# Instance norm over 65,536 rows: loads and stores moved to one queue in one fixed order, rows computed one by one

The kernel runs on one core of one Trainium2 chip. The metric is the device time of one execution in microseconds (us), lower is better. All runs quoted are fast-state runs. The engines are named as the profiler does: SP (SyncE) and ACT (ScalarE) issue transfers, DVE (VectorE) computes the statistics, ACT normalises; the 16 DMA engines move the data.

## The reference

```python
def reference(x, eps):                     # x: 256 x 256 x 4096, float32; eps = 1e-5
    mean = np.mean(x, axis=2, keepdims=True)
    var = np.var(x, axis=2, keepdims=True)
    return ((x - mean) / np.sqrt(var + eps)).astype(np.float32)
```

1.07 GB are read and 1.07 GB written; arithmetic per element is small.

## The kernel before

256 tiles of 128 partitions x 2 rows x 4096 (4 MB). Six buffers (192 KB of each partition). Loads are issued by SP, stores by ACT, so they stand in two DMA queues.

```python
    P, K, BUFS = 128, 2, 6
    io = ...tile_pool(name="io", bufs=BUFS)
    small = ...tile_pool(name="small", bufs=2 * BUFS)
    # ... (cut: shapes, eps_tile)
    for i in range(ntiles):
        x_tile = io.tile([P, K, d], mybir.dt.float32)
        nc.sync.dma_start(out=x_tile, in_=x_t[i])
        # ... (cut: small tiles)
        for r in range(K):
            for j in range(nsub):                         # 8 pieces of 512
                nc.vector.bn_stats(out=stats[:, r, j, :], in_=xr[:, r, j, :])
            nc.vector.bn_aggr(out=mv[:, r, :], in_=stats[:, r])
        nc.scalar.activation(out=rstd, in_=mv[:, :, 1], func=Sqrt, bias=eps_tile, scale=1.0)
        nc.vector.reciprocal(out=rstd, in_=rstd)
        nc.vector.scalar_tensor_tensor(out=nbias, ...)    # -mean * rstd
        for r in range(K):
            nc.scalar.activation(out=x_tile[:, r, :], in_=x_tile[:, r, :], func=Identity,
                                 bias=nbias[:, r : r + 1], scale=rstd[:, r : r + 1])
        nc.scalar.dma_start(out=out_t[i], in_=x_tile)
```

The order of the source need not be the order on an engine: in this kernel's trace the reciprocal of tile 1 stands behind 12 statistics of tile 2.

## Time and profile before

| | before |
|---|---|
| median, range | 5180.1 us, 5177.9 to 5187.5 |
| DMA engines, share of the span taken by packets | 99.2% |
| DVE, ACT busy | 51%, 38% |
| mean rate over 200 to 5000 us | 416 GB/s |
| a transfer, issue to landing (median) | load 23.7 us, store 18.6 us |
| packets' time beyond 1213 ns each, mean of an engine | 164 us |

A tile must be moved in and out: 16 packets of 32,768 bytes on each of the 16 DMA engines. At 1213 ns a packet that is 19.4 us per tile. Before, a tile takes 20.2 us. The prediction reads the rest of this profile. The last row of the table comes from the trace's packet records. One more quantity, which the prediction did not look at, will matter: a transfer's landing is told by 16 semaphore steps, read here as one from each engine (8192 steps and 8192 four-byte packets for 512 transfers). The time from the first step to the last is called the *spread* here. In the kernel before its median is 1.4 us and its largest value 5.1 us, so the engines go in step.

These are the two lines of the DMA issues (from issue to landing in the last column):

```profile
x_tile<-in_x_dram SPq DMA_DIRECT2D x256, 4096.0 KB, 23.7
out_dram<-x_tile ACTq DMA_DIRECT2D x256, 4096.0 KB, 18.6
```

A 4 MB transfer alone takes 9.7 us of packets, and two that share the engines some 19.4. So each queue holds little more than the one transfer that is moving.

### The profile page before, as it was taken

How to read it: one execution, taken by the hardware profiler on the slowest of the kernel's cores; microseconds unless marked ns; L12 is line 12 of the kernel's file. 1: busy time of each engine (PE TensorE's matmuls, PEld its weight loads, DVE VectorE, ACT ScalarE, POOL GpSimd, SP SyncE). 2: the span in 40 equal slices, each digit the busy share in tenths (PEclk: the TensorE clock that was granted, in tenths of full speed). 3: DMA queues.
4: the chain of work that ended last, by engine and by line, in shares of the span. 5: the costliest groups of instructions: out<-in, count | busy, mean ns of one | idle time of the engine just before them, and what ended most of it. 6: DMA issues, size and time to landing. Idle time of an engine off the chain costs nothing.

```text
span 5180.7 us, 7450 instructions
## 1 busy us (share of the span) xinstructions
DVE 2654.0 (51%) x5121; ACT 1967.0 (38%) x769; POOL 0.2 (0%) x4
## 2 busy tenths in 40 slices
DVE  6544555554455555444555554455555445555543
ACT  3333333433333433433343433333343333334334
POOL 0000000000000000000000000000000000000000
DMA  9999999999999999999999999999999999999998
GB/s 425 412 410 413 420 417 422 417 414 416 410 416 413 417 418 414 413 412 417 417 416 418 413 414 418 410 417 420 417 415 417 417 413 417 417 419 415 415 416 367
DMA packets 73786, 2147.99 MB, mean 415 GB/s; under 512 B 8192, under 2 KB 8192, under 8 KB 8192
## 3 DMA queue, kind: packets, MB, share of 16 engines
q1 hardware_dynamic: 36864, 1073.76, 49.7%
q10 hardware_dynamic: 36864, 1073.76, 49.5%
q14 instruction: 58, 0.48, 0.0%
HBM read 1073.74 MB, written 1073.74 MB: 415 GB/s over the span
## 4 chain that ended last, share of the span: by engine, by line
DMA 69%; DVE 17%; ACT 7%; issue 6%; another core or an unknown queue 0%; SPq 0%
DMA x_tile<-in_x_dram 43%; DMA out_dram<-x_tile 26%; DVE stats L55 16%; ACT x_tile L77 7%; DVE mv L56 1%; DVE nbias L67 0%; SPq L46 0%; DVE rstd L65 0%; ACT rstd L58 0%
## 5 line engine op out<-in xcount | busy, mean ns | idle before, releaser
L55 DVE BATCH_NORM_STATS2 stats<-x_tile 128x6 f32<-128x512 f32 x4096 | 2464.1, 674 | 2460.3 <-DMA x_tile<-in_x_dram 2460.3
L77 ACT ACTIVATE x_tile<-x_tile,nbias,rstd 128x4096 f32<-128x4096 f32 x512 | 1917.8, 3793 | 3172.3 <-DVE nbias L67 3172.3
L56 DVE BATCH_NORM_AGGREGATE mv<-stats 128x2 f32<-128x48 f32 x512 | 185.7, 363 | 8.8
L58 ACT ACTIVATE rstd<-mv,eps_tile 128x2 f32<-128x2 f32 x256 | 71.7, 280 | 23.9 <-DVE mv L56 23.9
L67 DVE SCALAR_TENSOR_TENSOR nbias<-mv,rstd 128x2 f32<-128x2 f32 x256 | 41.0, 160 | 8.8
L65 DVE RECIPROCAL rstd<-rstd 128x2 f32<-128x2 f32 x256 | 27.7, 108 | 23.6 <-ACT rstd L58 23.6
L58 ACT ACT_TABLE_LOAD x1 | 1.3, 1283 | 0.7 <-PEq L101 0.7
L42 DVE MEMSET eps_tile<- 128x1 f32 x1 | 0.1, 59 | 0.8 <-PEq L101 0.8
L101 POOL MEMSET const-bfloat16-1.0<- 128x1 bf16 x1 | 0.1, 101 | 0.0
L101 POOL MEMSET const-uint8-127<- 128x1 uint8 x1 | 0.1, 101 | 0.0
L101 POOL MEMSET const-float32-0.0<- 128x1 f32 x1 | 0.1, 98 | 0.2 <-issue 0.2
L101 POOL MEMSET const-float32-1.0<- 128x1 f32 x1 | 0.1, 98 | 0.0
## 6 DMA issues: line engine op xcount, KB each, us to landing
x_tile<-in_x_dram SPq DMA_DIRECT2D x256, 4096.0 KB, 23.7
out_dram<-x_tile ACTq DMA_DIRECT2D x256, 4096.0 KB, 18.6
```

Of the source, the lines that this page charges most:

```text
L42: nc.vector.memset(eps_tile, eps)
L55: nc.vector.bn_stats(out=stats[:, r, j, :], in_=xr[:, r, j, :])
L56: nc.vector.bn_aggr(out=mv[:, r, :], in_=stats[:, r])
L58: nc.scalar.activation(out=rstd, in_=mv[:, :, 1], func=mybir.ActivationFunctionType.Sqrt, bias=eps_tile, scale=1.0,)
L65: nc.vector.reciprocal(out=rstd, in_=rstd)
L67: nc.vector.scalar_tensor_tensor(out=nbias, in0=mv[:, :, 0], scalar=-1.0, in1=rstd, op0=mybir.AluOpType.mult, op1=mybir.AluOpType.mult,)
L77: nc.scalar.activation(out=x_tile[:, r, :], in_=x_tile[:, r, :], func=mybir.ActivationFunctionType.Identity, bias=nbias[:, r : r + 1], sca ...
L101: nc = _bacc.Bacc("TRN2", target_bir_lowering=False, num_devices=1)
```

## The change

Its intent: one queue (SP's) for everything, in the fixed order store i, load i+4, so that directions alternate in 4 MB blocks and a load never waits for the store just issued. Sqrt, reciprocal and bias are done row by row.

```diff
+    AHEAD = 4
-    small = ...tile_pool(name="small", bufs=2 * BUFS)
+    small = ...tile_pool(name="small", bufs=8)
-    for i in range(ntiles):
+    def load(i):
         x_tile = io.tile([P, K, d], mybir.dt.float32)
         nc.sync.dma_start(out=x_tile, in_=x_t[i])
+        tiles[i] = x_tile
+    def row(x_tile, r):       # one row: 8 bn_stats, bn_aggr, sqrt, reciprocal, nbias, identity
+        ...                   # (cut: the same operations on [P, 1] in place of [P, K])
+    def finish(i):
+        x_tile = tiles.pop(i)
         for r in range(K):
-            ...
-        nc.scalar.dma_start(out=out_t[i], in_=x_tile)
+            row(x_tile, r)
+        nc.sync.dma_start(out=out_t[i], in_=x_tile)
+    for i in range(AHEAD):
+        load(i)
+    for i in range(ntiles):
+        finish(i)
+        if i + AHEAD < ntiles:
+            load(i + AHEAD)
```

More of the change, by code (lines that the diff above doesn't have):

```diff
@@ L25 @@
     n, d = x_flat.shape
-    rows_per_tile = P * K
-    assert n % rows_per_tile == 0
-    ntiles = n // rows_per_tile
+    ntiles = n // (P * K)
+    assert n == ntiles * P * K
     x_t = x_flat.rearrange("(t p k) d -> t p k d", p=P, k=K)
     out_t = out_flat.rearrange("(t p k) d -> t p k d", p=P, k=K)
-    BN_FMAX = nc.vector.BN_STATS_FMAX
-    nsub = (d + BN_FMAX - 1) // BN_FMAX
-    assert d % BN_FMAX == 0
+    FMAX = nc.vector.BN_STATS_FMAX
+    nsub = d // FMAX
+    assert d == nsub * FMAX
     io = ctx.enter_context(tc.tile_pool(name="io", bufs=BUFS))
-    small = ctx.enter_context(tc.tile_pool(name="small", bufs=2 * BUFS))
+    small = ctx.enter_context(tc.tile_pool(name="small", bufs=8))
     singles = ctx.enter_context(tc.tile_pool(name="singles", bufs=1))
@@ L42 @@
     nc.vector.memset(eps_tile, eps)
-    for i in range(ntiles):
+    tiles = {}
+    def load(i):
         x_tile = io.tile([P, K, d], mybir.dt.float32)
         nc.sync.dma_start(out=x_tile, in_=x_t[i])
-        stats = small.tile([P, K, nsub, 6], mybir.dt.float32)
-        mv = small.tile([P, K, 2], mybir.dt.float32)
-        rstd = small.tile([P, K], mybir.dt.float32)
-        nbias = small.tile([P, K], mybir.dt.float32)
+        tiles[i] = x_tile
+    def row(x_tile, r):
         xr = x_tile.rearrange("p k (s f) -> p k s f", s=nsub)
-        for r in range(K):
-            for j in range(nsub):
-                nc.vector.bn_stats(out=stats[:, r, j, :], in_=xr[:, r, j, :])
-            nc.vector.bn_aggr(out=mv[:, r, :], in_=stats[:, r])
+        stats = small.tile([P, nsub, 6], mybir.dt.float32)
+        mv = small.tile([P, 2], mybir.dt.float32)
+        rstd = small.tile([P, 1], mybir.dt.float32)
+        nbias = small.tile([P, 1], mybir.dt.float32)
+        for j in range(nsub):
+            nc.vector.bn_stats(out=stats[:, j, :], in_=xr[:, r, j, :])
+        nc.vector.bn_aggr(out=mv, in_=stats)
         nc.scalar.activation(
             out=rstd,
-            in_=mv[:, :, 1],
+            in_=mv[:, 1:2],
             func=mybir.ActivationFunctionType.Sqrt,
@@ L68 @@
             out=nbias,
-            in0=mv[:, :, 0],
+            in0=mv[:, 0:1],
             scalar=-1.0,
@@ L74 @@
         )
-        for r in range(K):
-            nc.scalar.activation(
-                out=x_tile[:, r, :],
-                in_=x_tile[:, r, :],
-                func=mybir.ActivationFunctionType.Identity,
-                bias=nbias[:, r : r + 1],
-                scale=rstd[:, r : r + 1],
-            )
-        nc.scalar.dma_start(out=out_t[i], in_=x_tile)
+        nc.scalar.activation(
+            out=x_tile[:, r, :],
+            in_=x_tile[:, r, :],
+            func=mybir.ActivationFunctionType.Identity,
+            bias=nbias,
+            scale=rstd,
+        )
+    def finish(i):
+        x_tile = tiles.pop(i)
+        for r in range(K):
+            row(x_tile, r)
[6 more added lines that the diff above has]
+            load(i + AHEAD)
 _INS = ['x', 'eps']
```

## The prediction

> **What bounds the kernel now.** I read the front page first: busy shares, the DMA rows, the queues.
>
> ```profile
> DVE 2654.0 (51%) x5121; ACT 1967.0 (38%) x769; POOL 0.2 (0%) x4
> ...
> q1 hardware_dynamic: 36864, 1073.76, 49.7%
> q10 hardware_dynamic: 36864, 1073.76, 49.5%
> ```
>
> No compute engine is near its limit. The two DMA queues (q1 the loads, q10 the stores) hold the 16 DMA engines for 49.7 + 49.5 = 99.2% of 5180.7 us. The kernel is bound by DMA time, so it can gain only if packets take less time or if the last 0.8% of idleness goes. Bytes do not change: 256 tiles x 4 MB (4,194,304 bytes), each way.
>
> Then the DMA engines' rate by stretches (columns: stretch, length, DVE busy, ACT busy, POOL busy, clock, DMA share, GB/s).
>
> ```profile
> 13.00:31.00 18.00, 17.55 (x33) 7.30 (x3) 0.00 (x0) 1.00 1.01 437
> 5141.00:5165.00 24.00, 0.65 (x4) 22.00 (x8) 0.00 (x0) 1.00 1.02 437
> 200.00:5000.00 4800.00, 2456.91 (x4740) 1823.76 (x714) 0.00 (x0) 1.00 1.00 416
> ```
>
> The first stretch holds loads alone, the second stores alone; both ran at 437 (short windows round this up a little). The long middle runs at 416 with the engines as busy. So packets take longer there, and I went to the packet records of the trace. There are 65,536 packets of 32,768 bytes. In the loads-only and the stores-only stretch nearly all take 1213 ns (stores 1213 to 1254). Over the whole run they sum to 5132.5 us per engine, against 65,536 / 16 x 1.213 = 4968.4 us at 1213 ns each: 164 us too many. The other 48 us of the span are idle: start, end and slivers.
>
> **Where the 164 us arise.** I sorted the packets from 200 to 5000 us by the mix around them (stores as a share of the packets that start within 1.25 us). Half-and-half mixes average 1221 ns, so alternating directions packet by packet costs almost nothing. The long ones are where the mix changes: with 2 to 20% stores the mean is 1438 to 1480 ns, with 90 to 98% it is 1350. By event, counting excess within 2.6 us of a transfer's first packet:
> - a load that starts while only stores run (98 times): 0.871 us
> - a store that starts while only loads run (139 times): 0.346 us
> - a store that starts in a mix (20 times): 0.484 us
> - a load that starts while loads run (79) or in a mix (61), and a store that starts while stores run (79): 0.005 to 0.055 us
>
> The rule I read from it is that a transfer whose queue was EMPTY pays and a transfer that follows another in its own queue doesn't. The very first load agrees: its first 16 packets took 1614 to 2204 ns and its second 16 some 1236. Every time a queue goes empty and is filled again, that price is paid.
>
> Why queues go empty shows in the chain of waits and the queue's own waits:
>
> ```profile
> 2008.51 25.50 DMA x_tile<-in_x_dram
> 2034.03 5.44 DVE stats L55 x9
> ...
> SPq L46 <- DMA out_dram<-x_tile: 4914.6, 248, 33.2
> ```
>
> Each load is issued only when the store that frees its buffer has landed, about one per 20 us, and lands some 24 us later. All six buffers are taken; tile 246 has its statistics at 4949.8 us but is normalised from 5010.8, three tiles behind, so buffers sit waiting for ACT while DMA queues hold one transfer each.
>
> **What the Trainium skill says.**
> - "DMA: Bandwidth & Descriptors", section Where 436 GB/s comes from: a ceiling of 435.2 GB/s. The trace agrees: 16 x 32,768 / 1.213 us = 432.2 GB/s. So 4968 us is close to the floor for any order of transfers.
> - Same page, section Issuing engines are not separate DMA queues: whoever issues, the same 16 engines do the work. Agrees: both queues fill one 99.2%. It means that moving stores to SP takes nothing away in itself.
> - Same page, section Two DMAs through the same engine are not ordered: descriptors of one queue start in order but are pipelined, with separate read and write sides. Agrees for one direction (loads back to back show flat 1213 ns packets, 13 to 31 us). No case of a load behind a store in one queue exists in this trace.
> - "Perfetto Trace Analysis", section DMA Optimizations, suggests one issuing engine for inputs and another for outputs. The change does the opposite. No trace here compares them yet.
>
> **The change, part by part.**
>
> Order and depth. Four loads go ahead, then store i, load i+4, store i+1, ... on one queue. Load i+4 takes the buffer of tile i-2, whose store was issued two tiles earlier, not just now. When load i lands, the queue still holds store i-3, load i+1, store i-2, load i+2, store i-1: five transfers of 8 packets x 1.213 = 9.7 us, 48 us. Load i+3 follows when store i-3 lands, 9.7 us later. Store i needs tile i's compute. By the listed durations that is two rows of 8 x 0.60 us (the step between statistics; 5.4 us for nine) + 0.36 us, plus 0.28 + 0.11 + 0.16 us and about 0.4 us of handing over, plus the second row's 3.79 us: some 16 us. So the queue never falls below about four transfers (39 us), the engines never starve, and no queue is ever refilled from empty.
>
> Compute. Sqrt, reciprocal and the bias product become one per row: 256 more of each. ACT: 256 x 0.28 = 72 us more, 2039 in all. DVE: 256 x (0.108 + 0.160) = 69 us more, plus at most 512 short waits of 0.4 us for ACT, 205: 2654 + 69 + 205 = 2928. Both are below 60% of the span and off the path. Issues: SP issues 512 at 0.33 us = 169 us, nothing.
>
> The sum. 4968 (packets at 1213 ns) + 5 (the 8192 four-byte packets, 4.6 us per engine) + 1.7 (first packet starts) + 0.8 (first load's slow packets) + 1.5 (last packet to landing: the trace's median) = 4977. The tail shrinks too: before, the engines stood nearly idle from about 5125 to 5140 us, because the last four tiles were normalised only then. After, stores 252 to 254 (29 us) cover the compute of tile 255. I add 0.055 us (the worst of the cheap cases) for each of 512 transfers, 28 us: 5005. I predict **5010 us**, 3.3% less.
>
> **The rivals.**
>
> R1: the price is of turning direction, not of an empty queue. In the trace both came together, since queues are one-directional: this is the main doubt. The change turns direction twice in every tile, so it would pay 256 x (0.871 + 0.346) = 312 us: 4977 + 312 = 5290, 2.1% slower. If only the turn from store to load costs (a read from HBM started late): 256 x 0.871 = 223, so 5200, the same. Against: half-and-half mixes turn at every packet and show 1221 ns, and load after load in a queue shows that the next packet is fetched early. For: there, two queues could each fetch ahead on its own.
>
> R2: the written order isn't the order that runs. The instructions before stand by readiness as the compiler saw it, not by program order: the reciprocal of tile 1 stands after 12 statistics of tile 2. If the two spare buffers let loads 4 and 5 overtake store 0, the order becomes store i, load i+6, and load i+6 needs store i landed. SP then stops until the queue is empty, each tile: 1.5 us (last packet to landing) + 1.0 (issue to first packet) + 0.8 (slow first packets) = 3.3 us, 256 x (19.4 + 3.3) = 5810 us, 12% slower. Against: tile 1's reciprocal came so late because tile 1's sqrt stands behind store 0 on ACT, as if that store held its queue for about 10 us (12 statistics). If that is what the compiler assumed of every 4 MB issue, SP is full in its eyes and takes store 0 first whenever it is ready. I give R2 about one in ten.
>
> R3: nothing changes, because HBM itself turns slowly whichever queue asks, or because SP, waiting for compute, holds back loads: 5100 to 5200. The 16 us against 39 us of backlog speaks against the second.
>
> **Range and chances.** About 0.64 for the full gain or most of it (4975 to 5077), 0.2 for a price of 0.4 to 1.2 us per tile that eats it (5077 to 5285), 0.16 for the full price in both directions or R2. The range 4970 to 5300 holds the first, the second and R1 at its middle value.
>
> **What would show it right or wrong.** Right: one hardware queue with all 2147 MB; DMA share still about 1.00 in the middle but 430 GB/s or more; packets flat near 1213 ns at every change of direction; SP waits more for ACT and stores, yet a load's time from issue to landing rises to 40 us or more, since it lies behind others; loads and stores alternate on SP from load 4 on. Wrong by R1: share 1.00, but one long packet per engine at each turn, 0.3 to 0.9 us. Wrong by R2: six loads first and gaps of 2 to 4 us in every tile, DMA share near 0.87.

## The result, and the profile after

| | before | after |
|---|---|---|
| median, range (4 runs each) | 5180.1, 5177.9 to 5187.5 | 5059.6, 5015.6 to 5081.9 |
| ratio | | 0.9736, 95% interval 0.9673 to 0.9799 |
| runs | 5187.5, 5179.3, 5180.9, 5177.9 | 5015.6, 5081.9, 5077.9, 5041.4 |

A ratio here is the mean time of one kernel's fast runs over that of the other's in the same rounds, so it isn't quite the ratio of the medians. The kernel is faster, but it now scatters by 1.3%, where the kernel before scatters by 0.2% in these four runs. (In later rounds on two chips 7 of 26 runs of the kernel before took 5211 to 5231 us, counted as fast; none was profiled, so what made them longer is not known.) The profiled run is the changed kernel's fastest, 5015.6.

From the front page of that run:

```profile
DVE 2723.6 (54%) x5633; ACT 2069.7 (41%) x1025; POOL 0.2 (0%) x4
...
GB/s 422 431 432 433 433 433 432 433 434 434 433 433 433 433 432 434 433 433 433 433 433 432 434 433 433 432 433 433 433 433 433 433 433 432 434 433 419 416 422 305
...
q1 hardware_dynamic: 73728, 2147.52, 99.6%
...
x_tile<-in_x_dram SPq DMA_DIRECT2D x256, 4096.0 KB, 48.8
out_dram<-x_tile SPq DMA_DIRECT2D x256, 4096.0 KB, 53.3
```

One queue carries all bytes. Transfers land some 50 us after their issue, as four or five stand ahead of each. The rate is 433 GB/s for nine tenths of the run, then falls to about 419. The packets' excess over 1213 ns fell from 164 to 19 us per engine, in spite of some 500 changes of direction. On SP stand loads 0 to 3, store 0, load 4, store 1, load 5, as written.

The new thing is the spread. In the profiled run (from the semaphore steps of the trace):

```
at us      12   700  1400  2100  2800  3500  4200  4540  4900
spread us  0.5  8.1 13.2  18.1  23.2  28.2  34.0  38.1  38.5
```

Each DMA engine works through its own part of the queue, and nothing brings them together again. It is mainly one engine that falls behind: at 3000 us 14 of the 16 steps lie within 5.3 us, the next comes at 10.8 and the last at 24.8. The leading engine needs 19.36 us a tile, which is 16 packets without a gap (one each 1210 ns). The last engine needs 19.51. When the spread reaches 38 us, it stops growing, and both take 20.2 us a tile, as in the kernel before. Seen as stretches of the profile (columns: stretch, length, DVE, ACT and POOL busy, clock, DMA share, GB/s):

```profile
1000.00:2000.00 1000.00, 546.83 (x1129) 412.05 (x204) 0.00 (x0) 1.00 1.00 433
3500.00:4500.00 1000.00, 547.87 (x1134) 412.78 (x206) 0.00 (x0) 1.00 1.00 433
4550.00:4900.00 350.00, 186.40 (x384) 137.35 (x68) 0.00 (x0) 1.00 1.00 417
```

No engine stands idle in the slow stretch (share 1.00). Its packets are longer: 9% of them take 1.70 us on average, while from 1000 to 2000 us all but 0.1% take 1.21 to 1.26 us. The same trace shows how near to empty the leading engine's queue comes. From 1000 to 2000 us a load was issued 25.5 us (median) before the leading engine's step for the transfer in front of it. From 4550 to 4900 us that was 2.2 us, less than the 2.5 us that the prediction counts from last packet to landing and from issue to first packet.

### The profile page after: what moved, and what is told of

Same layout as the page of the kernel before. It is cut to its first block, busy times and chain, and to the rows that moved or that the text cites.

```text
span 5013.8 us, 8481 instructions
## 1 busy us (share of the span) xinstructions
DVE 2723.6 (54%) x5633; ACT 2069.7 (41%) x1025; POOL 0.2 (0%) x4
## 2 busy tenths in 40 slices
DMA packets 73794, 2148.06 MB, mean 428 GB/s; under 512 B 8192, under 2 KB 8192, under 8 KB 8192
## 3 DMA queue, kind: packets, MB, share of 16 engines
q1 hardware_dynamic: 73728, 2147.52, 99.6%
## 4 chain that ended last, share of the span: by engine, by line
DMA 76%; DVE 17%; another core or an unknown queue 4%; ACT 2%; issue 0%; SPq 0%
DMA x_tile<-in_x_dram 75%; DVE stats L58 16%; ACT x_tile L76 2%; DMA out_dram<-x_tile 1%; DVE mv L59 1%; DVE nbias L68 0%; DVE rstd L67 0%; ACT rstd L60 0%; SPq L88 0%; SPq L48 0%
## 5 line engine op out<-in xcount | busy, mean ns | idle before, releaser
L58 DVE BATCH_NORM_STATS2 stats<-x_tile 128x6 f32<-128x512 f32 x4096 | 2497.7, 676 | 2070.5 <-DMA x_tile<-in_x_dram 2070.5
L76 ACT ACTIVATE x_tile<-x_tile,nbias,rstd 128x4096 f32<-128x4096 f32 x512 | 1945.6, 3800 | 341.9 <-DVE nbias L68 336.5
L60 ACT ACTIVATE rstd<-mv,eps_tile 128x1 f32<-128x1 f32 x512 | 146.8, 287 | 2577.1 <-DVE mv L59 2577.1
L67 DVE RECIPROCAL rstd<-rstd 128x1 f32<-128x1 f32 x512 | 77.9, 152 | 173.2 <-ACT rstd L60 172.9
L68 DVE SCALAR_TENSOR_TENSOR nbias<-mv,rstd 128x1 f32<-128x1 f32 x512 | 77.4, 151 | 8.7
```

The source lines that it names most:

```text
L58: nc.vector.bn_stats(out=stats[:, j, :], in_=xr[:, r, j, :])
L60: nc.scalar.activation(out=rstd, in_=mv[:, 1:2], func=mybir.ActivationFunctionType.Sqrt, bias=eps_tile, scale=1.0,)
L68: nc.vector.scalar_tensor_tensor(out=nbias, in0=mv[:, 0:1], scalar=-1.0, in1=rstd, op0=mybir.AluOpType.mult, op1=mybir.AluOpType.mult,)
```

## The experiments

**Theories.** T (drift): while all engines have work queued, a tile costs 19.4 to 19.5 us. The last engine falls further and further behind the leading one, and a load can be issued only when the last engine has finished an old store. So the leading engine can be ahead by at most what stands in the queue, some 39 us here. From then on the leaders find their queues empty, and the old price returns. T2 (place): the slow stretch belongs to the end of the run. E: a queue that was empty pays. F: it is the single queue that matters. G: it is the depth of what is queued that matters, and the number of queues is nothing.

All ratios are against the kernel before in the same rounds.

| run | what | median us (runs) | range | ratio (95%) |
|---|---|---|---|---|
| after_again | unedited | 5059.1 (4) | 5010.5 to 5076.5 | 0.9709 (0.9639 to 0.9779) |
| ahead3 | 3 loads ahead | 5093.3 (4) | 5066.3 to 5102.2 | 0.9781 (0.9725 to 0.9838) |
| ahead5 | 5 loads ahead | 5150.6 (8) | 5145.9 to 5167.1 | 0.9923 (0.9892 to 0.9954) |
| sync32 | level start each 32 tiles | 5050.6 (4) | 5048.5 to 5053.8 | 0.9708 (0.9650 to 0.9766) |
| two_queues | stores from ACT | 5193.1 (12) | 5190.8 to 5198.0 | 0.9998 (0.9979 to 1.0017) |
| whole_tile | both rows together | 5009.5 (4) | 4998.5 to 5022.2 | 0.9631 (0.9585 to 0.9678) |
| before_sp | before, stores from SP | 5324.8 (4) | 5324.7 to 5325.3 | 1.0245 (1.0206 to 1.0284) |
| ahead6 | 6 loads ahead | 5919.9 (2) | 5919.6 to 5920.1 | 1.1390 (1.1323 to 1.1457) |
| two_queues_pinned | two queues, no lag | 5145.9 (4) | 5139.0 to 5146.3 | 0.9923 (0.9907 to 0.9940) |
| sync128 | level start once | 5016.8 (4) | 5009.7 to 5019.2 | 0.9676 (0.9662 to 0.9691) |
| whole_tile_again | as whole_tile | 5023.3 (4) | 4998.0 to 5036.4 | 0.9685 (0.9655 to 0.9716) |
| after_third | unedited | 5069.9 (4) | 5062.2 to 5081.0 | 0.9783 (0.9764 to 0.9802) |

The first four ran together, so did the next four, and so did the last four.

### after_again: the changed kernel, no edit

> The changed kernel once more, unedited. Its first four runs lay between 5015.6 and 5081.9 us, the kernel before within 0.2%. Theory T (drift): the 16 DMA engines run through the one queue each at its own pace, nothing brings them together again, the spread between the first and the last engine to finish one transfer grows steadily (0.5 us at the start, 18 us at 2069 us, 38 us at 4527 us in the profiled run), and when it reaches the depth of the queue (about 38 us) the leading engines find their queues empty and a tile takes 20.1 us again in place of 19.5. Then a run is long when the drift is fast: expected median 5015 to 5085, and in the profiled run the spread where packets get long is again 36 to 39 us, whatever the time at which it comes. Rival T2 (place): the slow stretch belongs to the late part of the run, from about 4500 us on (tiles 232 to 255, the last 9% of the addresses), whatever the spread.

Its profiled run took 5076.5 us. The spread passed 36 us at 3215 us, not at 4531. Tiles took 19.57 us up to there and 20.23 after it.

```profile
1000.00:2000.00 1000.00, 542.64 (x1122) 412.99 (x205) 0.00 (x0) 1.00 1.00 433
3300.00:3800.00 500.00, 262.36 (x545) 201.99 (x100) 0.00 (x0) 1.00 1.00 414
```

The slow stretch began some 1300 us earlier at the same spread, so T2 falls: it isn't the place in the run.

### ahead3 and ahead5: the depth of the queue

```diff
-    AHEAD = 4
+    AHEAD = 3        # ahead3; 5 in ahead5
-        nc.sync.dma_start(...)
+        tc.keep_in_program_order(nc.sync.dma_start(...))   # loads and stores
```

> Three loads ahead in place of four, order on the queue pinned. By T the smallest backlog falls to about 23 us (39 us of transfers when load i lands, less 16 us of compute until store i comes), so the spread can grow to about 23 us only, reached at some 2800 us with the drift of the first profile; from there 20.1 us per tile in place of 19.5: 5015 + (4500 - 2800) x 3.2% = 5070, range 5060 to 5120. T2: no change against the changed kernel in time, spread grows past 30 us, slow from 4500 us on.

> Five loads ahead in place of four (same six buffers), order pinned. Load i+5 now waits for store i-1 to land, with only load i+4 and store i behind it: a backlog of two transfers, 19.4 us. By T the spread stops at about 19 us, reached at some 2200 us, then 20.1 us per tile: 5015 + (4500 - 2200) x 3.2% = 5090, range 5075 to 5135, although more loads are ahead. T2, or a plain view that more loads ahead are better: 5015 to 5080, no slow stretch before 4500 us.

In ahead3 the spread reached 23 us at about 2450 us and stayed there to the end (largest value 24.1); tiles then took 20.0 us in place of 19.5. In ahead5 it reached 18 us at about 1250 us and stayed between 16.5 and 19.3 (half of the time 17.5 to 18.4); tiles then took 20.1 to 20.3, 20.25 on average.

```profile
500.00:1000.00 500.00, 271.78 (x561) 204.00 (x102) 0.00 (x0) 1.00 1.00 433
2000.00:3000.00 1000.00, 528.25 (x1094) 398.06 (x198) 0.00 (x0) 1.00 1.00 414
```

These two lines are of ahead5. The ceilings came out as worked out beforehand for 3 and 5 loads ahead: 23 and 19 us expected, 23 and 18 measured. (For 4 loads the queue's depth gave 39; the 38 of the first profile had been seen before theory T was made.) Ahead5 is slower than I had put it (5150.6 against 5075 to 5135). About half of that is the drift, which reached 18 us at 1250 us, not at 2200 (in the first profile at 2074); the other half is the slow tile, 20.25 us where I had taken 20.1. One more load ahead makes the kernel worse: load i+5 must wait for a store that was issued only one tile ago, so less stands behind it.

### sync32 and sync128: letting the engines start level again

```diff
-        x_tile = io.tile([P, K, d], mybir.dt.float32)
+        b = free.pop(-1 if sync else 0)      # the buffer free longest, or the one just stored
+        x_tile = bufs[b].tile([P, K, d], mybir.dt.float32, name="x_tile")
...
-            load(i + AHEAD)
+            load(i + AHEAD, sync=i % SYNC == SYNC - 1)   # SYNC = 32, or 128
```

(Order pinned as above.) At a sync, the load needs the buffer of the store just before it, so all 16 engines run dry once.

> The changed kernel, but after each 32 tiles one load takes the buffer of the store just issued, so that the queue runs empty once on all engines and they start level again (7 times). By T the spread falls to under 1 us each time, never passes 10 us, and no stretch is slow: 256 x 19.5 us + 7 x 3.3 us (1.5 landing + 1.0 to the first packet + 0.8 slow first packets) + 9 us of ends = 5024 us, and runs agree within 0.4%, unlike those of the changed kernel. T2: the last 9% stay slow and 23 us are lost: 5035 to 5105 with the same scatter as the changed kernel.

> As sync32, but the queue runs empty once only, after tile 127. Sync32 cost (5050 - 5004) / 7 = 6.5 us a time, where 5004 is 256 x 19.5 + 12. Spread before the one level start 20 to 30 us, after it the same growth again, never 36: no slow stretch, 4992 + 12 + 6.5 = 5011 us, range 5000 to 5025, runs within 0.3% if the drift is no faster than seen. If the drift were not what makes the changed kernel scatter: 5010 to 5085 like it.

In sync32 the spread never passed 9.2 us, the last 500 us ran at 432 GB/s, and the four runs lie within 5.3 us (0.1%):

```profile
4500.00:5000.00 500.00, 275.24 (x569) 204.91 (x102) 0.00 (x0) 1.00 1.00 432
```

T holds and T2 is out again. But it took 5050.6, not 5024. An undisturbed run is 256 x 19.5 + 12 = 5004 us, so a level start cost about (5050.6 - 5004) / 7 = 6.7 us (6.5 in the expectation of sync128), twice my 3.3. The trace shows what I had left out. While the engines are level, the last one loses time at loads that follow a store. In the profiled run of the changed kernel it lost 0.1 to 0.9 us at nearly every load up to 360 us, and hardly anything afterwards.

In sync128 the spread was 28 us before the one level start, 7 us some 600 us after it, and 21 us near the end. Its median is 53 us lower than that of the changed kernel beside it, after_third. Its range is 9.5 us, that of after_third 18.8 (0.4%): the scatter of 1% that I had expected there did not come. Up to the level start its spread grew as in after_third (18.5 and 17.4 us at 1190 us), so the new buffers by themselves show no effect on the drift.

```profile
1000.00:2000.00 1000.00, 542.74 (x1122) 413.39 (x205) 0.00 (x0) 1.00 1.00 433
3500.00:4900.00 1400.00, 761.34 (x1575) 580.63 (x287) 0.00 (x0) 1.00 1.00 433
```

The second line holds the place where the unedited kernel falls to 414 to 417; here is after_third:

```profile
4000.00:4900.00 900.00, 476.52 (x985) 357.09 (x178) 0.00 (x0) 1.00 1.00 416
```

So the spread's ceiling is shown to be what costs the time, and one drained queue in 256 tiles is enough to stay clear of it.

### ahead6: an empty queue in every tile

```diff
-    AHEAD = 4
+    AHEAD = 6        # order pinned as in ahead3
```

> Six loads ahead, order pinned: load i+6 needs the buffer of store i, which stands just before it, so all engines' queues run empty once in every tile. This is the prediction's R2, made on purpose: the engines stand still for 1.5 us (last packet to landing) + 1.0 (issue to first packet) and the first packets are 0.8 us longer: 256 x (19.4 + 3.3) = 5810 us, DMA share about 0.87, spread under 1.5 us. If draining costs nothing beyond the waiting of leading engines: 5000 to 5200.

```profile
1000.00:2000.00 1000.00, 458.60 (x950) 349.52 (x175) 0.00 (x0) 1.00 0.91 361
```

5919.9 us: (5919.9 - 4977) / 256 = 3.7 us a tile in place of 3.3. Packets were 450 us longer than 1213 ns each, 1.76 us a tile, and the engines stood still for 1.9 us a tile. So my idle term (2.5) was too large and the term of slow first packets (0.8) too small. The spread's median was 0.6 us. A drained queue keeps the engines in step and costs more than any drift.

### two_queues and two_queues_pinned: is it the single queue?

```diff
-        nc.sync.dma_start(out=out_t[i], in_=x_tile)
+        nc.scalar.dma_start(out=out_t[i], in_=x_tile)
```

> The changed kernel with its stores issued from ACT, as before, and nothing else changed: loads alone on SP's queue. Compute keeps up here, so loads can stand several deep in their queue, but each store finds its own queue empty. By theory E (a queue that was empty pays, 0.35 to 0.48 us for a store that joins loads or a mix in the kernel before) a tile takes 19.4 + 0.35 to 0.48 = 19.8 to 19.9 us, about 5080 to 5110 us, with engines more in step than on one queue. Rival F (only the single queue matters): as the kernel before, 5160 to 5190. Rival G (only the order and depth matter, the number of queues is nothing): as the changed kernel, 5010 to 5085 with a spread that grows to 30 us and more.

It took 5193.1 us, as the kernel before, which looks like F. But the test was spoiled. With a store on ACT the compiler again put ACT's work of a tile about three tiles behind its statistics: tile 121's statistics ended at 2418 us and its normalising began at 2474. The buffers stood waiting, and the queues were as shallow as before:

```profile
x_tile<-in_x_dram SPq DMA_DIRECT2D x256, 4096.0 KB, 23.8
out_dram<-x_tile ACTq DMA_DIRECT2D x256, 4096.0 KB, 21.1
```

So I pinned every DVE and ACT instruction to program order, with nothing else changed:

```diff
-            nc.vector.bn_stats(...)
+            pin(nc.vector.bn_stats(...))     # pin = tc.keep_in_program_order; likewise all others
```

> Two queues as in two_queues, but every DVE and ACT instruction pinned to program order, which takes away the lag of three tiles with which the compiler had put it back (a tile was normalised some 70 us after its statistics), so that loads can now stand up to four deep. Theory E (a queue that was empty pays): only the stores find theirs empty, 0.15 to 0.48 us per tile by the two kernels' events: 19.6 to 19.9 us per tile, 5020 to 5110 us. F (one queue for both is what matters): 5160 to 5195. G (depth alone): 5000 to 5085 with a spread that grows.

```profile
1000.00:2000.00 1000.00, 561.73 (x1126) 420.62 (x206) 0.00 (x0) 1.00 1.00 433
3000.00:4000.00 1000.00, 527.68 (x1057) 396.87 (x193) 0.00 (x0) 1.00 0.99 407
...
x_tile<-in_x_dram SPq DMA_DIRECT2D x256, 4096.0 KB, 58.8
out_dram<-x_tile ACTq DMA_DIRECT2D x256, 4096.0 KB, 43.5
```

Two queues with several transfers waiting ran at the same 433 GB/s and 19.5 us a tile for some 2400 us, with the same growing spread. F falls for this stretch, and so does my form of E, which wanted a price at every store. The slow stretch began when the spread had reached about 20 us, and tiles then took 20.65 us. The stores' queue had run out first: up to then a store was issued with at least 23 us still in front of it for the last engine, a load with 38. The spread did not stop at 20 us, as T in its simple form would have it: within some 200 us it jumped to about 45 us for loads and 32 for stores and stayed there. How that comes about is not shown. The total, 5145.9, lies outside all three expectations, since none of them had counted an earlier slow stretch with two queues. So G has the mechanism of the fast stretch: what matters is that something is always queued. What the single queue brings is a slow stretch that begins later (at 38 us of spread against about 20) and costs less (20.2 us a tile against 20.65), and an order that the compiler left as written; beside it, in the same rounds, the changed kernel took 5069.9 us.

### before_sp: the queue alone, in the kernel before

```diff
-        nc.scalar.dma_start(out=out_t[i], in_=x_tile)
+        nc.sync.dma_start(out=out_t[i], in_=x_tile)
```

> The kernel before with one word changed: its stores are issued from SP. The compiler then orders the queue in threes: loads 3, 4, 5, stores 3, 4, 5, loads 6, 7, 8 and so on. A store comes 18.5 us after its load lands and the two loads behind it last 19.4 us, so the queue hardly ever holds more than one transfer when a store comes: backlog about 1 us. By E the turn into stores pays about once in three tiles or more often, small gaps come on top, and the engines stay in step (spread under 3 us): 19.5 to 20.0 us per tile, 5010 to 5130. Rival F (one queue is all that matters): the same as the changed kernel, with the spread growing.

```profile
q1 hardware_dynamic: 73728, 2147.52, 95.2%
...
x_tile<-in_x_dram SPq DMA_DIRECT2D x256, 4096.0 KB, 30.7
out_dram<-x_tile SPq DMA_DIRECT2D x256, 4096.0 KB, 11.1
```

It is slower than the kernel before. The order is three loads, three stores, as I had read. A store lands 11.1 us after its issue, so nothing stood ahead of it: the queue was empty when it came. Stores 96, 97 and 98 were issued at 2018.9, 2029.8 and 2040.6 us, that is at DVE's pace of 10.8 us a tile, while a store's packets last 9.7. I had not counted that step and expected 19.5 to 20.0 us a tile; it took 20.7. A single queue by itself is no gain.

### whole_tile, and after_third beside it: the rows

```diff
-        for r in range(K):
-            row(x_tile, r)
+        tile_all(x_tile)       # statistics of both rows, then one sqrt, reciprocal, nbias
```

> The changed kernel with the statistics of a tile's two rows first and then one sqrt, one reciprocal, one bias product for both, as before. Store i comes some 18.5 us after load i lands in place of 16. The smallest backlog is still the four transfers (39 us) just before load i+3, so by T and E nothing changes: 5010 to 5085, the spread's limit again 36 to 39 us. Rival: row by row is what brought it, since it gave the compiler's order without the lag of three tiles; then 5150 to 5190.

> whole_tile once more, beside the changed kernel on the same chip. If its 5009 us against 5059 came from the drift of that chip and hour, both have the same median within 25 us here; if the row-by-row arithmetic itself costs something (smaller instructions do not touch the DMA queue by any theory here), whole_tile is again 40 to 50 us faster.

> The changed kernel once more, on the chip of sync128 and whole_tile_again. By T 5005 to 5085, and its runs scatter by 1% where sync128's do not; the time at which the profiled run's spread passes 36 us fits its length: (5060 - that time) x 3.2% is what it lost against 5004.

Row by row isn't what brought the gain: without it the kernel is faster, 5009.5 and 5023.3. On one chip and in the same rounds its runs (4998.0 to 5036.4) lie below all of the changed kernel's (5062.2 to 5081.0). My expectation of 25 us at most failed; the other branch, 40 to 50 us faster, came true (46.5). The traces show the way: whole_tile's spread passed 36 us at 4271 and 4028 us, after_third's at 3215. In after_third tiles took 19.57 us before and 20.20 after: (5060 - 3215) / 20.2 = 91 tiles x 0.70 = 64 us, and 0.07 us for each of the 164 tiles before, 11 us: 75 over the 5004 of an undisturbed run, which is 5079 where 5074.2 was measured (the 3.2% of the expectation give 5063).

**Why the last engine falls behind.** The DMA row "instruction" holds fetches of 8192 bytes, 0.31 us each:

```profile
q14 instruction: 66, 0.54, 0.0%
```

That is the changed kernel; whole_tile and the kernel before have 58. In the profiled run of the changed kernel, from 500 to 4200 us, I compared how long the last engine takes for two transfers with 19.36 us. With no fetch in that time: no more (-0.01 us, 287 cases). With one fetch: 0.60 us more on average (88 cases). With two: 0.97 us (5 cases). Not every fetch hits the last engine. Those that do come every 107 to 118 us, 113 on average, and cost it 0.8 to 1.0 us each: at 19.5 us and 22 DVE instructions a tile that is one for each 128 DVE instructions. In whole_tile, with 20 DVE instructions a tile, they come every 116 to 137 us, 125 on average: 128 instructions again. In the changed kernel's run the last engine lost 26.8 us in that stretch, the leading one 0.06, and the fetches account for it. So the steady drift goes with fetches that come once in 128 DVE instructions. This is read from coincidence in the traces; no run took the fetches away.

A second loss is not explained. In after_again, after_third, ahead5 and sync128 the spread jumped from about 11 to 18 us between 800 and 1250 us (in after_third with 0.6 to 0.8 us lost at most loads). In whole_tile and its repeat a slower jump came later, from 12 or 13 us to 19 or 20 between 1190 and 1780 us. In the first profiled run and in ahead3 none came there. So why whole_tile is faster is explained only in part: at 3140 us its repeat stood at 28.1 us, after_third at 34.5, and one fetch in 125 us in place of 113 is worth some 2.4 of these 6.4 us (an estimate, at 0.9 us each). The first profiled run, with 22 DVE instructions a tile, drifted more slowly than either trace of whole_tile (36 us at 4531 against 4271 and 4028). That fewer instructions make the drift slower is therefore not shown.

## Why the prediction was right, point by point

- **The bound.** Right. The DMA engines stayed at 99.6% and the gain came from shorter packets: 164 us of excess became 19.
- **The order.** Right. SP carries loads 0 to 3, then store i, load i+4. R2 didn't happen by itself; made on purpose (ahead6) it cost 3.7 us a tile, 5919.9 us where I had 5810.
- **R1, the price of a turn.** Wrong as a rule: some 500 turns on one queue, and the excess is 19 us in place of 312. A remnant is there while the engines are level.
- **An empty queue pays.** It led near the right number. What the runs support is more careful: whenever the queues stay filled, packets are flat (the changed kernel, two_queues_pinned up to 2400 us); whenever queues run empty, they are not (before, before_sp, ahead6, every run past its ceiling). The part played by lone transitions of direction isn't separated, and why the last engine, whose own queue is full, slows down along with the starving ones stays open.
- **The cause of empty queues before.** I had named the lag of three tiles only as a sign of full buffers. two_queues against two_queues_pinned shows that it is the cause there: with it 5193 (ratio 0.9998 to the kernel before), without it 5146 (0.9923) and 433 GB/s for the first half. The kernel before itself was not run with its order pinned.
- **"The queue never falls below about four transfers (39 us), the engines never starve."** The 39 us were right, the conclusion was not. It holds for the last engine only; the others eat the 39 us up as they run ahead of it. This is the term missing from the sum. It is worth 0 to 75 us a run, it made the median 5059.6 where I said 5010, and it brought the scatter. The run with the slowest drift, 5015.6, comes closest to the sum.
- **The sum's last term.** Right in size by luck. Its 28 us stood for slow first packets, but in the fast stretch packets are 0.008 us a tile over 1213 ns, 2 us a run. What fills the place is the last engine, which needs 19.51 us a tile where 16 packets of 1213 ns are 19.41: some 26 us a run that the sum, a mean over the engines, did not contain. The 5 us from 5005 to 5010 have no working. The listed compute times add up to 15.1 us, not 16; the trace has 15.3 us from a load's landing to the issue of its store.
- **The tail.** Half right: stores cover the last compute, but the engines end apart, and the last slice shows 305 GB/s.
- **Compute and waits.** DVE: 2723.6 us busy and 173 us of waits for ACT before the reciprocal, 2897 together; 2928 predicted. ACT 2069.7, 2039 predicted. Both off the path, as said. Of the signs, SP's longer waits came for ACT alone (1341 us); for stores they fell from 4915 to 3413 us.

## What to carry to other kernels

For a kernel bound by DMA time, ask how many transfers stand queued at each moment, not which engine issues them: compare issue to landing with the time of one transfer's packets, and let a load reuse a buffer whose store was not issued just now (here, with six buffers, two stores back had a lower median than none, one or three). Look at the order in which the compiler really placed the work, since a lag between two engines uses up buffers as surely as a small pool does. If times begin to scatter, look at the spread between the first and the last DMA engine of a transfer, and let the queue drain once before the spread reaches the queue's depth.

## What the Trainium skill lacked or had wrong

- "DMA: Bandwidth & Descriptors" says that nothing orders DMAs across the 16 engines; it doesn't say that on a queue kept full one can fall ever further behind. Here the spread grew from 0.5 to 38 us in 3200 to 4500 us and then cost some 0.7 us a tile (19.5 to 20.2).
- The same page's list of queue rows names row 14 as internal, and "Runtime: NRT & Kernel Launch", section Instruction fetch mechanics, calls the cost of a fetch mostly hidden; neither says what a fetch costs the transfers beside it. Here an 8192-byte instruction fetch came with 0.8 to 1.0 us of delay on the engine that fell behind.
- The same page says that issuing from several engines only saves issue time. In rate that agreed while both queues were deep (433 GB/s either way); the spread at which the slow stretch began did not (38 us on one queue, about 20 on two), and in it a tile took 20.2 and 20.65 us.
- "Perfetto Trace Analysis", section DMA Optimizations, says that separate issuing engines for inputs and outputs may make sense. Here that was 5145.9 us with pinned order, against 5069.9 on one queue in the same rounds, and 5193.1 without pinning, in other rounds.
- No page gives a price for letting a queue of SP run empty between large transfers; the fixed cost of one DMA in "DMA: Bandwidth & Descriptors" is fitted for the path of GpSimd. Here the price was 3.7 us each time when paid in every tile, and about 6.7 us each time when paid every 32 tiles.
